# The gains of q and k as one column each, applied in the split of k behind its transpose

## The chip, the core and the metric

The kernel runs on one core of a Trainium2 chip, in one launch. The metric is the device time of one execution in microseconds (us). The engines are PE (TensorE, with a separate row for its weight loads, PEld), DVE (VectorE), ACT (ScalarE), POOL (GpSimd) and SP (SyncE, which here issues DMAs). PE's granted clock is full over the whole span.

## The reference, cut to what matters

One decoder layer: a modulated RMSNorm of x, a projection h @ w_in, two groups of attention heads, gates, an output projection and a residual. 512 tokens, model width 1024, head width 64, 8 query heads in each group A and B, 2 key heads in each branch.

```
def qk_norm(t, gain):
    tf = t.astype(jnp.float32)
    return tf * lax.rsqrt(jnp.mean(tf * tf, -1, keepdims=True) + EPS) * gain

qa = qk_norm(heads(q_a, A_HEADS), q_gain_a) * qscale       # qscale = 64 ** -0.5
ka = qk_norm(heads(k_a, A_KV), k_gain_a)
qb = qk_norm(heads(q_b, B_HEADS), q_gain_b) * qscale
k_cmp = qk_norm(compress_blocks(heads(kc, B_KV), ...), k_gain_cmp)
k_sel = qk_norm(heads(ks, B_KV), k_gain_sel)
k_win = qk_norm(heads(kw, B_KV), k_gain_win)
```

Only products of q and k are used afterwards (logits = q . k), so the gain of q, the gain of k and qscale can be put together as one vector of 64 numbers for each kind of key: four vectors, for window keys of group A, selected, window and compressed keys of group B. The kernel calls them kg and multiplies them into k alone.

## The kernel before, in words

All matrices are float32. For the large products the kernel splits each operand into a high part, rounded to the type float32r, and a low part (value minus high), and sums three products (high by high, high by low, low by high). ACT writes the high part, DVE subtracts to make the low part.

*Stage one, up to about 59 us.* x is loaded transposed, its norm and the modulation are made, and the projections of q, k, v of group A run on PE, k block by k block, while SP streams their weights through rings of four buffers (`ada_ring`, `wst_ring`). Between the loads of the first four blocks and those of the last four SP issues one load of small constants, the tile `rest` (L315). The instructions of this stage are held in the order in which they are written (`in_order`); at its end DVE makes `kg` from the gains (L429 to L434) and the negated sinks `nsink` (L435).

*Stage two.* The other projections (kv_cmp, kv_sel, kv_win_g, q_b, then the z gates) run on PE as a stream of small units, and between them stand slots of attention: scores (`slot_scores`, L882), a maximum and exponential (DVE L887, ACT L894), a scaling, a transpose (L930, L940), and the product with v (L957). The matrix instructions of the slots and of the compression MLP are chained in a fixed order. For the rest the compiler's planner decides at compile time, from estimated costs, in which order each engine issues what it has; the order in the trace is therefore not the written order everywhere.

*The keys.* `k_scale` is called three times: for group A (ty 0, tile kT), for selected keys (ty 1) and window keys (ty 2, both in tile kTb). Its input has tokens on partitions. DVE multiplies by the reciprocal norm of each token and head (L548), then by kg (L550), PE transposes four blocks of 128 tokens into one bank of PSUM, so that the 64 dimensions of head group 0 lie on partitions 0 to 63 and those of group 1 on 64 to 127 (L554). For each group ACT writes the high part twice (L558), once on its own half of the partitions and once on the other, and DVE writes the low part twice (L560). 64 partitions by 512 columns each. In the trace the second group's ACT copies begin when the first group's DVE subtractions are through. `q_scale` does the same for q without a gain (L531 to L542).

*The compressed keys.* In `cmp_mlp` one DVE instruction multiplies the output of the MLP in PSUM by its reciprocal norm and by kg (L650), PE transposes it (L654), and DVE copies it out of PSUM into kTc (L656).

Behind stage two come the remaining slots with the z gates and then the output projection (L1028 to L1039), which PE ends.

Of the kernel before, what the change touches and what calls it, by code (L numbers as in the profile page):

```python
# [9 lines left out]
F32 = mybir.dt.float32  # L10
# [3 lines left out]
AF = mybir.ActivationFunctionType  # L14
OP = mybir.AluOpType
# [4 lines left out]
S, D, HD, NB = 512, 1024, 64, 4  # L20
# [61 lines left out]
def hybrid_layer_kernel(ctx, tc, A, out):  # L82
    nc = tc.nc
    PE, DVE, ACT, POOL, SP = nc.tensor, nc.vector, nc.scalar, nc.gpsimd, nc.sync
# [3 lines left out]
    con = ctx.enter_context(tc.tile_pool(name="con", bufs=1))  # L88
# [22 lines left out]

    first = con.tile([128, 168], F32, name="first")
    cT, prm, ident = first[:, 0:8], first[:, 8:40], first[:, 40:168]
    rest = con.tile([128, 960], F32, name="rest")
    sml, anti = rest[:, 0:416], rest[:, 416:544]
    pos = rest[:, 544:576].rearrange("p (a b) -> p a b", a=2)
    w2 = rest[:, 576:832].rearrange("p (a b d) -> p a b d", a=2, b=2)
    cmask = rest[:, 832:960].rearrange("p (a b) -> p a b", a=NB)
    qga, kga, qgb, kgs, kgw, kgc = (sml[:, 64 * i:64 * i + 64] for i in range(6))
    bnsa, sinks = sml[:, 384:408], sml[:, 408:416]  # L120
    ones = con.tile([128, 1], F32, name="ones")
    DVE.memset(ones, 1.0)

# [1 line left out]
    hl = [T2(F32R, f"hl{k}") for k in range(8)]  # L125
    gacc = con.tile([128, D], F32, name="gacc")
    line_d = dram.tile([2, 8, LINE], F32, name="line_d")
    kg = con.tile([128, 4, HD], F32, name="kg")
    nsink = con.tile([128, 8], F32, name="nsink")
    sc_col = con.tile([128, 8], F32, name="sc_col")  # L130
    prm1 = con.tile([128, 8], F32, name="prm1")
# [43 lines left out]
    def split_to(g, p, ahead):  # L175

        while split_done[0] < min(len(split_list), split_pos[g, p] + ahead + 1):
            n, q = split_list[split_done[0]]
            if not all((n, h) in raws for h in ((0, 1) if n in COL else (q // 2,))):
                break  # L180
            split(n, q)
            split_done[0] += 1
# [115 lines left out]
    with in_order(tc) as begun:  # L298
# [113 lines left out]
        for k in range(8):  # L412
# [6 lines left out]
            for n in range(3):  # L419
# [6 lines left out]
                    new_tile(m)  # L426
                if k >= 6 and n == 1:
                    split_to("kv_cmp", 2 * (k - 6) + 1, 0)
        DVE.tensor_tensor(kg[:, 0], qga, kga, op=OP.mult)  # L429
        DVE.tensor_tensor(kg[:, 1], qgb, kgs, op=OP.mult)  # L430
        DVE.tensor_tensor(kg[:, 2], qgb, kgw, op=OP.mult)
        DVE.tensor_tensor(kg[:, 3], qgb, kgc, op=OP.mult)
        DVE.tensor_scalar(kg[:, 0:3], kg[:, 0:3], -(HD ** -0.5), None, op0=OP.mult)
        DVE.tensor_scalar(kg[:, 3], kg[:, 3], HD ** -0.5, None, op0=OP.mult)  # L434
        DVE.tensor_scalar(nsink, sinks, -1.0, None, op0=OP.mult)  # L435

    mp = ctx.enter_context(tc.tile_pool(name="mp", bufs=1))
# [1 line left out]
    def W2(name, shape=(128, 512)):  # L439
        return mp.tile(list(shape), F32, name=name, tag="w2", bufs=5)  # L440
# [22 lines left out]
    def PT():  # L463
        return ps_t.tile([128, 512], F32, name="pt")
# [31 lines left out]
    @contextmanager  # L496
    def block():

        with in_order(tc, chain, PE.engine) as last:
            yield  # L500
        chain.update(last)


    HALF = (slice(0, 64), slice(64, 128))
    qs = {}
    kT = {}
# [16 lines left out]
    def rnorm(ssq, n):  # L523
        DVE.tensor_scalar(ssq, ssq, 1.0 / HD, EPS, op0=OP.mult, op1=OP.add)
        return rsqrt(ssq, n)
# [19 lines left out]
    def k_scale(ty, src, rn):  # L545

        kn = W2("kn", (128, 8, HD))
        DVE.tensor_tensor(kn, src.rearrange("p t (g d) -> p (t g) d", d=HD), rn[:, :, None].to_broadcast([128, 8, HD]),  # L548
                          op=OP.mult)
        DVE.tensor_tensor(kn, kn, kg[:, ty:ty + 1, :].to_broadcast([128, 8, HD]), op=OP.mult)  # L550
        yield 0.0
        pt = PT()
        for t in range(NB):
            PE.transpose(pt[:, t * 128:(t + 1) * 128], kn[:, 2 * t:2 * t + 2].rearrange("p g d -> p (g d)"), ident)  # L554
        for g in range(2):
            part, k = pt[HALF[g], :], kT[ty, g]
            for e in (g, 1 - g):
                ACT.activation(k[HALF[e], 0, :], part, AF.Copy)  # L558
            for e in (g, 1 - g):
                DVE.tensor_tensor(k[HALF[e], 1, :], part, k[HALF[g], 0, :].bitcast(F32), op=OP.subtract)  # L560
        yield 0.44

    rn_a = {}
# [38 lines left out]
    def cmp_mlp():  # L602
        ph = ps_s.tile([128, 512], F32, name="s")
        for half in range(2):
            for _ in range(WAIT_M[half]):
                yield 0.0
            with block():
                for ii in range(8 * half, 8 * half + 8):
                    for kv in range(2):
                        PE.matmul(ph[64 * kv:64 * kv + 64, 0:256], X[kv][:, half, :, :, ii % 8].rearrange("p g n -> p (g n)"),  # L610
                                  raws[f"cmp{kv}", ii // 4][:, ii % 4, :], start=ii == 0, stop=ii == 15,
                                  skip_group_check=True)
                    if ii % 4 == 3:
                        load_next()
                        load_next()
            yield 3.6
        th_ = W2("cth", (128, 256))
        ACT.activation(th_, ph[:, 0:256], AF.Tanh, scale=0.5)
        sh = W2("csh", (128, 256))
        DVE.scalar_tensor_tensor(sh, th_, 1.0, ph[:, 0:256], op0=OP.add, op1=OP.mult)  # L620
        yield 0.0
        pt = PT()
        for hc in range(2):
            PE.transpose(pt[:, 128 * hc:128 * hc + 128], sh[:, 128 * hc:128 * hc + 128], ident)
        sT = W2("csT", (128, 2, 64))
        sTv = W2("csTv", (128, 2, 2, 4, 32))
        ptv = pt[:, 0:256].rearrange("p (c n) -> p c n", c=2)
        ACT.activation(sT, ptv[:, :, 0:64], AF.Copy, scale=0.5)
        for hc in range(2):
            DVE.tensor_scalar(sTv[:, hc], ptv[:, hc, 64:128].rearrange("p (g n) -> p g n", g=2)[:, :, None, :]  # L630
                              .to_broadcast([128, 2, 4, 32]), 0.5, None, op0=OP.mult)
        yield 0.25
        po = ps_s.tile([128, 512], F32, name="s")
        for hc in range(2):
            PE.matmul(po[0:64, 0:64], sT[:, hc, :], w2[:, 0, hc, :], start=hc == 0, stop=hc == 1)
        pv = ps_s.tile([128, 512], F32, name="s")
        for g in range(2):
            for hc in range(2):
                PE.matmul(pv[:, 64 * g:64 * g + 64], sTv[:, hc, g].rearrange("p r n -> p (r n)"), w2[:, 1, hc, :],
                          start=hc == 0, stop=hc == 1)  # L640
        for g in range(2):
            vc[g] = mp.tile([128, HD], F32, name=f"vc{g}")
            ACT.activation(vc[g], pv[:, 64 * g:64 * g + 64], AF.Copy)
        kcn = mp.tile([64, 2, HD], F32, name="kcn")
        sq = mp.tile([64, HD], F32, name="kcsq")
        ssk = sm.tile([128, 1], F32, name="ssk")
        DVE.memset(ssk, 1.0)
        ACT.activation(sq, po[0:64, 0:64], AF.Square, accum_out=ssk[0:64, :])
        rn = rnorm(ssk, 1)
        DVE.scalar_tensor_tensor(kcn, po[0:64, None, 0:64].to_broadcast([64, 2, HD]), rn[0:64, :],  # L650
                                 kg[0:64, 3:4, :].to_broadcast([64, 2, HD]), op0=OP.mult, op1=OP.mult)
        yield 1.3
        pt = PT()
        PE.transpose(pt[:, 0:64], kcn.rearrange("p a d -> p (a d)"), ident[0:64, 0:64])  # L654
        kTc = mp.tile([128, 2, 32], F32, name="kTc")
        DVE.tensor_copy(kTc.rearrange("p g n -> p (g n)"), pt[:, 0:64])  # L656
        yield 0.1
        X["kTc"] = kTc

# [283 lines left out]
    po = {}  # L943
# [84 lines left out]
    for n in range(8):  # L1028
        xr = mp.tile([128, S], F32, name="xr", tag="qc", bufs=2)
        ACT.dma_start(xr, A["xT"][n])  # L1030
        b = PJ()
# [10 lines left out]
def _layout(inp):  # L1042

    g = lambda n: np.asarray(inp[n])
    a = {}
    cc = np.ascontiguousarray
# [23 lines left out]
    for n, name in enumerate(("w_cmp_k1", "w_cmp_v1")):  # L1070
        a[f"w_cmp{n}"] = cc(g(name)[0].reshape(4, 4, 128, 256).transpose(0, 2, 1, 3))
    eye = np.eye(128, dtype=np.float32)
    a["first"] = cc(np.concatenate([g("c").reshape(8, 128).T, g("b_ada").reshape(24, 128).T,
                                    g("norm_gain").reshape(8, 128).T, eye], axis=1))
    smalls = np.concatenate([g(n)[0] for n in ("q_gain_a", "k_gain_a", "q_gain_b", "k_gain_sel", "k_gain_win",
                                               "k_gain_cmp", "b_nsa_gate", "sinks")])
    pos = np.stack([g("cmp_pos_k")[0].reshape(16, 128), g("cmp_pos_v")[0].reshape(16, 128)]).transpose(2, 0, 1)
    w2 = np.stack([g("w_cmp_k2")[0].reshape(2, 128, 64), g("w_cmp_v2")[0].reshape(2, 128, 64)]).transpose(2, 0, 1, 3)
    t = np.arange(S).reshape(NB, 128).T[:, :, None]
    cmask = np.where(16 * np.arange(32)[None, None, :] + 31 <= t, 0.0, -BIG).astype(np.float32)  # L1080
    a["rest"] = cc(np.concatenate([np.broadcast_to(smalls, (128, 416)), eye[::-1], pos.reshape(128, -1),
                                   w2.reshape(128, -1), cmask.reshape(128, -1)], axis=1))
    dist = 511 - np.arange(LINE)
    bucket = np.searchsorted(BUCKET_STARTS, np.maximum(dist, 0), side="right") - 1
# [25 lines left out]
```

## Time and profile before

| | us |
|---|---|
| median of 3 timed runs | 323.44 (322.80 to 324.18) |
| the profiled execution | 322.34 |
| its span, first to last instruction | 320.6 |
| PE busy in the span | 311.4 |
| PEld busy | 256.1 |
| DVE busy | 234.9 |
| ACT busy | 195.8 |

A row of the profile names a line of the kernel (L550), the engine, the operation, and output<-input by the program's names with partitions x elements. Weight loads (PEld) run beside the matrix instructions of PE. Matrix instructions are pipelined, so a busy PE is not PE at its peak. What stands in brackets in a timeline is the idle time of that engine just before the instruction and the instruction that ended the wait.

### The profile page before, as it was taken

Reading aid. Unit: us, or ns where it says so; the run is one execution under the profiler, and the core shown is the slowest. Engines: PE = TensorE matmul, PEld = TensorE weight load, DVE = VectorE, ACT = ScalarE, POOL = GpSimd, SP = SyncE. Lnnn points to the kernel's source line nnn. Section 1 sums busy time; section 2 is a strip of 40 time slices with the busy share of each in tenths; the row PEclk is TensorE's granted clock in tenths of the full one; section 3 lists DMA queues with packets and bytes.
Section 4 is the critical chain, followed back from the end, with each engine's and each line's share of the span. In section 5 each row is a group of like instructions: output and inputs, shape, how many; then the busy total and the mean of one; then the engine's idle time right before and its main releaser. Section 6 shows DMA issues by size and latency. Waiting matters only on the chain.

```text
span 320.6 us, 5999 instructions
## 1 busy us (share of the span) xinstructions
PE 311.4 (97%) x2187; PEld 256.1 (80%) x2188; DVE 234.9 (73%) x688; ACT 195.8 (61%) x473; POOL 4.5 (1%) x22
## 2 busy tenths in 40 slices
PE   6999999999999999999999999999999999999995
PEld 2477878888898899999975888788788878778884
DVE  2656797999995467797886999999599688454220
ACT  4566544957895667786956867877676866432100
POOL 1000000000000000000000000000000000000000
PEclk9999999999999999999999999999999999999999
DMA  7999998500085444130130223426224213243201
GB/s 264 385 408 410 378 325 265 171 0 3 0 252 176 130 167 131 35 113 20 39 127 4 97 65 102 133 66 196 68 67 132 66 67 131 67 140 114 108 33 65
DMA packets 31060, 44.26 MB, mean 138 GB/s; under 512 B 1766, under 2 KB 23398, under 8 KB 31032
## 3 DMA queue, kind: packets, MB, share of 16 engines
q1 hardware_dynamic: 29880, 41.79, 38.6%
q10 hardware_dynamic: 1152, 2.10, 2.1%
q8 instruction: 17, 0.28, 0.4%
q14 instruction: 11, 0.09, 0.1%
HBM read 41.74 MB, written 2.14 MB: 137 GB/s over the span
## 4 chain that ended last, share of the span: by engine, by line
PE 84%; DVE 6%; ACT 5%; DMA 2%; issue 1%; SPq 1%; POOL 0%; ACTq 0%; POOLq 0%
PE pj L491 30%; PE pj L481 9%; PE sq L294 8%; PE po L957 8%; PE s L882 7%; PE pt L940 4%; PE skv L295 4%; PE pt L930 3%; PE s L610 2%; DMA raw<-in_bias 2%; PE pj L227 2%; PE po L963 1%; DVE qs L542 1%; ACT pa L894 1%; PE pj L258 1%
## 5 line engine op out<-in xcount | busy, mean ns | idle before, releaser
L169 ACT ACTIVATE wh<-raw 128x512 fp32r<-128x512 f32 (+1 forms) x52 | 31.2, 635 | 16.4 <-PE pj L491 10.7
L170 DVE TENSOR_TENSOR wl<-raw,wh 128x512 fp32r<-128x512 f32 (+1 forms) x52 | 34.8, 690 | 8.2 <-ACT wh L169 4.7
L481 PE MATMUL pj<-wh,hh 128*128 128x256 f32 (+1 forms) x128 | 36.9, 288 | 0.0
L481 PE MATMUL pj<-wl,hh 128*128 128x256 f32 (+1 forms) x128 | 36.8, 287 | 0.0
L481 PE MATMUL pj<-wh,hl 128*128 128x256 f32 (+1 forms) x128 | 36.6, 286 | 0.0
L894 ACT ACTIVATE pp<-pp,nm 128x256 f32<-128x256 f32 (+2 forms) x48 | 29.4, 613 | 9.2 <-DVE nm L887 8.8
L491 PE MATMUL pj<-hh,wh 128*128 128x512 f32 x80 | 32.2, 403 | 0.0
L491 PE MATMUL pj<-hl,wh 128*128 128x512 f32 x80 | 31.9, 399 | 0.0
L491 PE MATMUL pj<-hh,wl 128*128 128x512 f32 x80 | 31.8, 397 | 0.0
L887 DVE CUSTOM_DVE_ANT_0 pp<-s,bias 128x256 f32<-128x256 f32 (+2 forms) x48 | 25.8, 547 | 2.4 <-PE s L882 2.4
L491 PE MATMUL pj<-yl,wh 128*128 128x512 f32 x64 | 25.4, 397 | 0.0
L491 PE MATMUL pj<-yh,wh 128*128 128x512 f32 x64 | 25.4, 401 | 0.0
L491 PE MATMUL pj<-yh,wl 128*128 128x512 f32 x64 | 25.3, 395 | 0.0
L481 PEld LDWEIGHTS pj<-wh,hh 128*128 128x128 f32 x128 | 24.2, 189 | 0.3 <-issue 0.2
L481 PEld LDWEIGHTS pj<-wl,hh 128*128 128x128 f32 x128 | 24.2, 189 | 0.2 <-issue 0.2
L481 PEld LDWEIGHTS pj<-wh,hl 128*128 128x128 f32 x128 | 24.2, 189 | 0.0
L882 PE MATMUL s<-kTb,qs 128*128 128x256 f32 (+2 forms) x96 | 23.7, 358 | 0.0
L1038 DVE SCALAR_TENSOR_TENSOR fin<-pj,gate,xr 128x512 f32<-128x512 f32 x8 | 6.0, 750 | 23.9 <-PE pj L491 23.9
L915 DVE TENSOR_SCALAR pp<-pp,rr,grev 128x256 f32<-128x256 f32 (+2 forms) x48 | 21.5, 475 | 0.3
L941 ACT COPY ptT<-pt 128x384 f32<-128x384 f32 (+1 forms) x32 | 15.7, 528 | 6.8 <-PE pt L940 6.6
L491 PEld LDWEIGHTS pj<-hh,wh 128*128 128x128 f32 x80 | 15.1, 188 | 4.7 <-issue 2.0
L931 ACT COPY ptT<-pt 128x512 f32<-128x512 f32 (+1 forms) x28 | 15.4, 551 | 4.7 <-PE pt L930 4.4
(235 smaller groups left out, 718.9 us busy)
## 6 DMA issues: line engine op xcount, KB each, us to landing
ada_ring<-in_w_ada_ss SPq DMA_DIRECT2D x16, 512.0 KB, 8.1
raw<-in_w_cmp SPq DMA_DIRECT2D x8, 512.0 KB, 6.3
raw<-in_w_gate SPq DMA_DIRECT2D x8, 512.0 KB, 4.8
raw<-in_w_o SPq DMA_DIRECT2D x8, 512.0 KB, 3.9
wst_ring<-in_w_qkv_a SPq DMA_DIRECT2D x8, 384.0 KB, 10.3
xTp<-in_xT SPq DMA_DIRECT2D x8, 256.0 KB, 4.6
xr<-in_xT ACTq DMA_DIRECT2D x8, 256.0 KB, 2.8
bias<-line_d SPq DMA_DIRECT2D x8, 256.0 KB, 4.3
```

The source lines that it names most:

```text
L169: ACT.activation(wh, src, AF.Copy)
L170: DVE.tensor_tensor(wl, src, wh.bitcast(F32), op=OP.subtract)
L294: PE.matmul(pj_q[tb], lt, w[:, 0:512], start=f, stop=l, skip_group_check=True)
L481: PE.matmul(bank[:, t * n:(t + 1) * n], h[:, tb * 128:(tb + 1) * 128], w[:, k % 2, :], start=k == 0 and m == 0, stop=k == 7 and m == 2)
L491: PE.matmul(bank, w, h, start=k == 0 and m == 0, stop=k == 7 and m == 2)
L882: PE.matmul(ps, qs[h][:, 128 * i:128 * i + 128], k[:, hl_, lo:lo + w], start=hl_ == 0, stop=hl_ == 1)
L887: DVE.tensor_tensor_reduce(out=P[:, g, 0:w], in0=ps, in1=bt, scale=1.0, scalar=init, op0=OP.add, op1=OP.min, accum_out=nm[:, g:g + 1])
L894: ACT.activation(P[:, g, 0:e], P[:, g, 0:e], AF.Exp, bias=nm[:, g:g + 1], scale=-1.0, accum_out=dn[:, g:g + 1])
L915: DVE.tensor_scalar(v, v, rr[:, g:g + 1], gates[:, g, br:br + 1], op0=OP.mult, op1=OP.mult)
L931: ACT.copy(T[:, :, 0:nb, :], rev(pt[:, 0:2 * nb * 128].rearrange("p (g b q) -> p g b q", g=2, b=nb)))
L941: ACT.copy(T[:, 0:nb, :], rev(pt[:, 0:nb * 128].rearrange("p (b q) -> p b q", b=nb)))
L957: PE.matmul(o[64 * g:64 * g + 64, 128 * i:128 * i + 128], vb[:, 64 * g:64 * g + 64], sl["T"][g][:, b, :], start=first_of and b == 0, stop= ...
```

## The change

The gains come as columns: the host lays `rest` out with 584 instead of 960 numbers for each partition, four columns of q gains and four of k gains, each the 64 gains twice, one copy for each half of the partitions. kg becomes four columns instead of four rows of 64 repeated on all partitions. Two small DVE instructions make it. In `k_scale` the multiplication L550 goes; the two ACT copies take the column as a scale for each partition, and the two DVE subtractions become (transposed value times column) minus high. In `cmp_mlp` the gain goes from the instruction ahead of the transpose into the copy behind it.

```diff
-    rest = con.tile([128, 960], F32, name="rest")
...
-    qga, kga, qgb, kgs, kgw, kgc = (sml[:, 64 * i:64 * i + 64] for i in range(6))
-    bnsa, sinks = sml[:, 384:408], sml[:, 408:416]
+    rest = con.tile([128, 584], F32, name="rest")
+    bnsa, sinks, qgain, kgain = rest[:, 0:24], rest[:, 24:32], rest[:, 32:36], rest[:, 36:40]
...
-    kg = con.tile([128, 4, HD], F32, name="kg")
+    kg = con.tile([128, 4], F32, name="kg")
...
-        DVE.tensor_tensor(kg[:, 0], qga, kga, op=OP.mult)
-        DVE.tensor_tensor(kg[:, 1], qgb, kgs, op=OP.mult)
-        DVE.tensor_tensor(kg[:, 2], qgb, kgw, op=OP.mult)
-        DVE.tensor_tensor(kg[:, 3], qgb, kgc, op=OP.mult)
-        DVE.tensor_scalar(kg[:, 0:3], kg[:, 0:3], -(HD ** -0.5), None, op0=OP.mult)
-        DVE.tensor_scalar(kg[:, 3], kg[:, 3], HD ** -0.5, None, op0=OP.mult)
+        for c, sign in ((slice(0, 3), -1), (slice(3, 4), 1)):
+            DVE.scalar_tensor_tensor(kg[:, c], qgain[:, c], sign * HD ** -0.5, kgain[:, c], op0=OP.mult, op1=OP.mult)
...
-        DVE.tensor_tensor(kn, kn, kg[:, ty:ty + 1, :].to_broadcast([128, 8, HD]), op=OP.mult)
...
-            part, k = pt[HALF[g], :], kT[ty, g]
+            part, by, k = pt[HALF[g], :], kg[HALF[g], ty:ty + 1], kT[ty, g]
             for e in (g, 1 - g):
-                ACT.activation(k[HALF[e], 0, :], part, AF.Copy)
+                ACT.activation(k[HALF[e], 0, :], part, AF.Copy, scale=by)
             for e in (g, 1 - g):
-                DVE.tensor_tensor(k[HALF[e], 1, :], part, k[HALF[g], 0, :].bitcast(F32), op=OP.subtract)
+                DVE.scalar_tensor_tensor(k[HALF[e], 1, :], part, by, k[HALF[g], 0, :].bitcast(F32),
+                                         op0=OP.mult, op1=OP.subtract)
...
-        DVE.scalar_tensor_tensor(kcn, po[0:64, None, 0:64].to_broadcast([64, 2, HD]), rn[0:64, :],
-                                 kg[0:64, 3:4, :].to_broadcast([64, 2, HD]), op0=OP.mult, op1=OP.mult)
+        DVE.tensor_scalar(kcn, po[0:64, None, 0:64].to_broadcast([64, 2, HD]), rn[0:64, :], None, op0=OP.mult)
...
-        DVE.tensor_copy(kTc.rearrange("p g n -> p (g n)"), pt[:, 0:64])
+        DVE.tensor_scalar(kTc.rearrange("p g n -> p (g n)"), pt[:, 0:64], kg[:, 3:4], None, op0=OP.mult)
...
+    gains = np.stack([g(n)[0] for n in ("q_gain_a", "q_gain_b", "q_gain_b", "q_gain_b",
+                                        "k_gain_a", "k_gain_sel", "k_gain_win", "k_gain_cmp")], axis=1)
```

## Rows read from the trace of the kernel before

**Rows 1.** Page, parts 1 and 4: busy us (share) x instructions; shares of the chain

```profile
PE 311.4 (97%) x2187; PEld 256.1 (80%) x2188; DVE 234.9 (73%) x688; ACT 195.8 (61%) x473; POOL 4.5 (1%) x22
...
PE 84%; DVE 6%; ACT 5%; DMA 2%; issue 1%; SPq 1%; POOL 0%; ACTq 0%; POOLq 0%
```

**Rows 2.** Stretch, length, busy us of PE, PEld, DVE, ACT, POOL; clock, DMA share, GB/s

```profile
0.00:58.00 58.00, 54.44 (x349) 39.30 (x351) 38.58 (x99) 31.77 (x54) 1.42 (x6) 1.00 0.96 345
58.00:160.00 102.00, 100.22 (x783) 91.16 (x782) 81.57 (x255) 76.43 (x201) 3.11 (x16) 1.00 0.30 92
58.00:76.00 18.00, 17.63 (x98) 14.80 (x97) 17.48 (x44) 12.49 (x27) 0.55 (x4) 1.00 0.16 50
76.00:94.00 18.00, 17.31 (x136) 16.11 (x135) 16.85 (x47) 16.10 (x45) 1.15 (x5) 1.00 0.27 70
130.00:138.00 8.00, 7.74 (x64) 7.29 (x63) 6.32 (x18) 7.41 (x19) 0.19 (x1) 1.00 0.00 0
```

**Rows 3.** What the weight load waited for, 58 to 160 us: us, times, longest

```profile
PEld s L882 <- DVE nm L887: 1.7, 6, 0.5
...
PEld pt L930 <- ACT kr L777: 0.8, 1, 0.8
PEld s L882 <- ACT qs L541: 0.6, 1, 0.6
PEld pt L554 <- DVE kn L550: 0.6, 2, 0.3
PEld pt L930 <- ACT wh L169: 0.4, 1, 0.4
...
PEld pt L536 <- DVE qn L531: 0.2, 1, 0.2
```

**Rows 4.** DVE groups by line and shape: count | busy us, mean ns | idle before

```profile
L1038 DVE SCALAR_TENSOR_TENSOR fin<-pj,gate,xr 128x512 f32<-128x512 f32 x8 | 6.0, 750 | 23.9 <-PE pj L491 23.9
...
L560 DVE TENSOR_TENSOR kTb<-pt,kTb 64x512 fp32r<-64x512 f32 x8 | 5.5, 688 | 1.0 <-ACT kTb L558 1.0
...
L550 DVE TENSOR_TENSOR kn<-kn,kg 128x512 f32<-128x512 f32 x3 | 2.1, 689 | 0.1
...
L816 DVE SCALAR_TENSOR_TENSOR yf<-po,szb 128x512 f32<-128x512 f32 x2 | 1.4, 691 | 5.0 <-PE po L963 5.0
...
L650 DVE SCALAR_TENSOR_TENSOR kcn<-s,n_y,kg 64x128 f32<-64x128 f32 x1 | 0.3, 342 | 0.0
...
L656 DVE COPY kTc<-pt 128x64 f32<-128x64 f32 x1 | 0.2, 224 | 0.8 <-PE pt L654 0.8
```

**Rows 5.** ACT groups by line and shape, the same columns

```profile
L917 ACT ACTIVATE pa<-pa,rr 128x256 f32<-128x256 f32 x12 | 6.1, 509 | 1.1 <-DVE rr L911 1.0
...
L558 ACT ACTIVATE kTb<-pt 64x512 fp32r<-64x512 f32 x8 | 4.7, 592 | 3.1 <-PE pt L554 2.2 <-DVE kTb L560 0.7
...
L337 ACT ACTIVATE sq<-xTp 128x256 f32<-128x256 f32 x2 | 0.7, 408 | 0.0
```

**Rows 6.** Timeline of DVE: start, us, instruction [idle before, releaser]

```profile
58.94 0.22 DVE L429 TENSOR_TENSOR kg<-rest 128x64 f32<-128x64 f32 x1
...
59.75 0.16 DVE L435 TENSOR_SCALAR nsink<-rest 128x8 f32<-128x8 f32 x1
...
103.56 1.40 DVE L560 TENSOR_TENSOR kTb<-pt,kTb 64x512 fp32r<-64x512 f32 x2 [0.80 <-ACT kTb L558]
```

**Rows 7.** Timeline of the weight load at the second and third split

```profile
98.40 0.42 PEld L554 LDWEIGHTS pt<-first,kn 128*128 128x128 f32 x4 [0.33 <-DVE kn L550]
...
105.73 0.30 PEld L882 LDWEIGHTS s<-kT,qs 128*128 128x128 f32 x2 [0.28 <-DVE nm L887]
...
131.07 0.42 PEld L554 LDWEIGHTS pt<-first,kn 128*128 128x128 f32 x4
```

**Rows 8.** DMA issues of rest: count, KB each, median us to landing

```profile
rest<-in_rest SPq DMA_DIRECT2D x1, 480.0 KB, 10.7
```

**Rows 9.** Timeline of ACT at the third split

```profile
130.37 0.60 ACT L794 ACTIVATE pp<-pj 128x512 f32<-128x512 f32 x1 [2.98 <-PE pj L481]
```

More of the change, by code (lines that the diff above doesn't have):

```diff
@@ L113, in hybrid_layer_kernel @@
     cT, prm, ident = first[:, 0:8], first[:, 8:40], first[:, 40:168]
-    rest = con.tile([128, 960], F32, name="rest")
[L115 to L118, printed above, removed]
-    qga, kga, qgb, kgs, kgw, kgc = (sml[:, 64 * i:64 * i + 64] for i in range(6))
-    bnsa, sinks = sml[:, 384:408], sml[:, 408:416]
+    rest = con.tile([128, 584], F32, name="rest")
+    bnsa, sinks, qgain, kgain = rest[:, 0:24], rest[:, 24:32], rest[:, 32:36], rest[:, 36:40]
+    anti = rest[:, 40:168]
+    pos = rest[:, 168:200].rearrange("p (a b) -> p a b", a=2)
+    w2 = rest[:, 200:456].rearrange("p (a b d) -> p a b d", a=2, b=2)
+    cmask = rest[:, 456:584].rearrange("p (a b) -> p a b", a=NB)
     ones = con.tile([128, 1], F32, name="ones")
@@ L1074, in _layout @@
                                     g("norm_gain").reshape(8, 128).T, eye], axis=1))
-    smalls = np.concatenate([g(n)[0] for n in ("q_gain_a", "k_gain_a", "q_gain_b", "k_gain_sel", "k_gain_win",
-                                               "k_gain_cmp", "b_nsa_gate", "sinks")])
+    smalls = np.concatenate([g("b_nsa_gate")[0], g("sinks")[0]])
+    gains = np.stack([g(n)[0] for n in ("q_gain_a", "q_gain_b", "q_gain_b", "q_gain_b",
+                                        "k_gain_a", "k_gain_sel", "k_gain_win", "k_gain_cmp")], axis=1)
     pos = np.stack([g("cmp_pos_k")[0].reshape(16, 128), g("cmp_pos_v")[0].reshape(16, 128)]).transpose(2, 0, 1)
@@ L1080, in _layout @@
     cmask = np.where(16 * np.arange(32)[None, None, :] + 31 <= t, 0.0, -BIG).astype(np.float32)
-    a["rest"] = cc(np.concatenate([np.broadcast_to(smalls, (128, 416)), eye[::-1], pos.reshape(128, -1),
+    a["rest"] = cc(np.concatenate([np.broadcast_to(smalls, (128, 32)), np.concatenate([gains, gains]), eye[::-1], pos.reshape(128, -1),
                                    w2.reshape(128, -1), cmask.reshape(128, -1)], axis=1))
```

## The prediction

> **What bounds the kernel now.** I read the page first, then the busy time by stretch, then what the weight load of PE waits for, then single instructions. On the page [rows 1] PE is busy for 97% of the span and carries 84% of the chain that ended last; DVE is at 73%, ACT at 61%. All that the change edits runs between 58 and 160 us, so that stretch counts. There [rows 2] PE is busy for 100.22 of 102 us, but within it two stretches are different: from 58 to 76 us DVE is busy for 17.48 of 18.00 us and from 76 to 94 for 16.85, so beside PE a second engine is full. After that DVE has room. The waits of the weight load in 58 to 160 us [rows 3] are short: 1.7 us on the minima of the scores (nm), 0.8 on an eviction (kr), 0.6 on qs, 0.6 on kn, 0.4 on a weight split (wh), 0.2 on qn, together 4.3 us. This is all that a faster k preparation can give back there, and a slower one adds to the same list. The reader is to see that a change worth a couple of microseconds on DVE is here worth at most what stands in that list.
>
> **The change, part by part.**
>
> *Gains (kg).* Six DVE instructions, from 58.94 to 59.75 us [rows 6], 0.81 us, become two on three columns and one column. A tiny instruction beside them (nsink, eight columns) takes 0.16 us [rows 6]; two make 0.32. DVE gives back 0.49 us, at a place where it is full.
>
> *Second multiplication of kn (L550).* Three instructions of 0.689 us each go [rows 4]: 2.07 us of DVE.
>
> *Low half of the split (L560).* Twelve subtractions of 0.688 us become a multiply and subtract with a scalar for each partition. No row has that form at 64 partitions. The nearest is fin: the same operation out of PSUM with such a scalar and a second tensor in SBUF, 512 columns, 0.750 us; without it, with a constant, yf out of PSUM takes 0.691 [rows 4]. So each costs between 0.00 and 0.06 us more. I take fin's form, 12 x 0.062 = 0.74 us.
>
> *High half (L558).* Twelve ACT copies of 0.592 us get a scale for each partition. The nearest pair, both 128x256 and out of SBUF: 0.509 us with such a scale (L917), 0.408 without (L337) [rows 5]. The difference, 0.101 us, is my value, none at all is the lower bound: 12 x 0.101 = 1.21 us of ACT. The copies read PSUM, which the pair does not; I see no row that says the scalar costs more there.
>
> *kcn and kTc.* One operand goes from the 0.342 us instruction, and the 0.224 us copy gets a scalar (0.06 by the above) [rows 4]: between -0.1 and +0.1 us, taken as nothing. It is one pair, and no row of it stands in the list of waits [rows 3].
>
> *The load of rest.* It shrinks from 480 KB [rows 8] to 584/960 of that, 292 KB. At the 345 GB/s of the first 58 us [rows 2] the 188 KB are 0.56 us of transfer. I cost it at nothing: PE is busy there for 54.44 of 58 us, and what it needs is loaded ahead into rings of four. If that cover is gone, it is a gain of up to 0.56 us. Nothing is moved past on the SP queue; the same number of DMAs is issued.
>
> Sum by engine: DVE -0.49 - 2.07 + 0.74 = -1.82 us, ACT +1.21 us.
>
> Now the path. The split of k is serial: two ACT copies, two DVE subtractions, for one head group, then the same for the other, since the second ACT pair starts behind the first DVE pair. The DVE row at 103.56 shows the hand-over from ACT, with 0.80 us of idle DVE [rows 6]. It grows by 4 x 0.101 + 4 x 0.062 = 0.65 us, and loses 0.69 us in front. So the last piece of k comes when it came before (-0.04), the first group's 0.69 - 0.20 - 0.12 = 0.37 us sooner. The three splits differ in what PE waits for.
>
> *First split (58 to 76 us).* DVE is full; it gives back 0.49 + 0.69 - 0.25 = 0.93 us. The waits that this can shorten are kn (0.2 of its 0.6), qn, qs and, through the DVE queue, kr [rows 3], 1.8 us. ACT is busy for only 12.49 of 18 us [rows 2], so its 0.4 us more are hidden there. I take -0.6, between 0 and -0.93; behind it the next late things are the qs splits, on DVE and ACT in turn.
>
> *Second split (94 to 106 us).* PE's wait of 0.33 us for kn at 98.40 goes [rows 7]. But at 105.73 PE waits 0.28 us for the minimum of the scores [rows 7], which stands in the DVE queue behind the last pair of the split, and that pair waits for ACT [rows 6]. From the first pair to the last that queue grows by 0.20 + 0.12 + 0.12 = 0.44 us. Net +0.1, between -0.33 and +0.44. This is where a gain is given back.
>
> *Third split (130 to 138 us).* Here the transpose at 131.07 waits for nothing [rows 7], so the removed 0.69 us is hidden already. ACT is busy for 7.41 of 8.00 us [rows 2], in a run that begins at 130.37 after 2.98 us of idle [rows 9], and at its end PE waits 0.4 us for wh [rows 3]. The split puts 4 x 0.101 = 0.40 us into that run. An earlier kn lets ACT start it sooner, so I take half: +0.2, between -0.2 and +0.5.
>
> Sum: -0.6 + 0.1 + 0.2 = -0.3 us. With the ends: 0 + 0.44 + 0.5 = +0.9 above, -0.93 - 0.33 - 0.2 - 0.56 = -2.0 below. The profiled execution took 322.34 us (span 320.6 and 1.74 around it); it would be 322.0. It lies below all three timed runs (322.80 to 324.18), so I set the difference against their median: 323.44 - 0.3 = 323.1 us.
>
> A rule that bears on which engine is the bound: the Trainium skill, Perfetto Trace Analysis, Identifying the Most-Contended Engine, says that the busy share of matmuls is a poor measure of PE, that the share of weight loads is the one to take, and that the engine with the highest share is to be optimised first. By it DVE leads in both stretches from 58 to 94 us, and its saving would count in full there. The traces so far bear this out in part: weight loads are busy for 14.80 and 16.11 of 18 us, less than DVE [rows 2].
>
> **The rivals.**
>
> *DVE paces the stage (faster).* Every DVE microsecond saved shortens the end: 323.44 - 1.82 = 321.6. For it: the DVE shares of 97 and 94% [rows 2]. Against: over 58 to 160 us DVE is busy for 81.57 of 102 us, and PE's waits on kn and qn are 0.8 us in all [rows 2, 3].
>
> *The split is the path (slower).* PE waits at the end of each split and what L550 gives back is lost before it (as in the third split, where PE comes later than kn). Then each split costs its 0.65 us: 3 x 0.65 = +1.95, 325.4 us. It decides where the nm wait behind each split grows by the whole 0.65; two splits of three give only +1.3. For it: the waits of 0.28 us at 105.73 and on wh [rows 3, 7]. Against: 0.69 us go from the same chain.
>
> *Another order.* The order of DVE and ACT behind 58 us is made at compile time from estimated costs; six groups of instructions change theirs, so it can come out differently, with other waits. Price: half of the 4.3 us [rows 3] gone or half again as much, 2.1 us: 321.3 or 325.5. The profile of before tells nothing of which.
>
> **How the numbers follow.** About 0.5%, 1.6 us, is what a measurement of this kernel can tell from no change. My forecast has 0.47 and a range of its own of 321.9 to 324.4. DVE as the pace has 0.20; at -1.82 it lies just past the limit, so 0.13 faster, 0.07 same. The split as the path has 0.08: 0.05 slower, 0.03 same. Another order has 0.25: 0.14 faster, 0.10 slower, 0.01 same. Together faster 0.27, same 0.47 + 0.07 + 0.03 + 0.01 = 0.58, slower 0.15. The range goes from 321.0 to 325.1, which takes in the rivals' near ends.
>
> **What would show it.** Right: L550 is gone; L558 stands near 0.69 us and L560 near 0.75; PE's waits on kn vanish at the first two splits; the nm wait behind the second split grows; DVE's busy time falls by about 1.8 us, ACT's rises by 1.2, PE's stays within a few tenths. Wrong: L558 or L560 unchanged in length, or the weight-load waits of 58 to 160 us changing by over 1.5 us in sum, which would be another order or DVE as the pace.

## The result, and the profile after

The changed kernel took 325.65 us (median of six runs, 324.64 to 327.00), the kernel before, run beside it, 323.79 us (322.80 to 325.87). The ratio is 1.0059, 95% interval 1.0030 to 1.0087: slower by 1.9 us, and above the predicted range. The profiled execution of the changed kernel took 326.35 us, its span is 324.3 us.

The prices of the single instructions came as worked out, and the time did not. First the pages and groups that answer to those of before. In the changed file most lines stand 1 to 6 lower: L560 is L554, L558 is L552, L169 is L168, L887 is L881, L930 is L924, L491 is L486.

The page of the changed kernel, parts 1 and 4 [rows 1]:

```profile
PE 315.5 (97%) x2187; PEld 257.6 (79%) x2188; DVE 233.9 (72%) x681; ACT 198.2 (61%) x473; POOL 4.5 (1%) x22
...
PE 73%; DVE 9%; ACT 7%; DMA 7%; issue 2%; SPq 1%; ACTq 0%
```

Its busy time by stretch, the columns of [rows 2], with one stretch more (10 to 20 us):

```profile
0.00:58.00 58.00, 54.73 (x337) 38.88 (x339) 36.56 (x95) 29.60 (x51) 1.42 (x6) 0.97 0.92 333
58.00:160.00 102.00, 100.33 (x780) 90.42 (x779) 78.96 (x243) 77.45 (x200) 3.10 (x16) 1.00 0.31 97
10.00:20.00 10.00, 8.21 (x49) 4.66 (x50) 5.71 (x21) 4.54 (x11) 0.00 (x0) 0.84 0.98 381
58.00:76.00 18.00, 17.68 (x93) 14.40 (x92) 17.30 (x40) 14.79 (x31) 0.43 (x3) 1.00 0.24 78
```

What its weight load waited for from 58 to 160 us [rows 3]:

```profile
PEld s L876 <- DVE nm L881: 2.3, 9, 0.3
...
PEld s L876 <- ACT qs L536: 0.5, 1, 0.5
PEld pt L924 <- ACT pa L911: 0.4, 1, 0.4
...
PEld pt L548 <- DVE kn L543: 0.2, 1, 0.2
PEld pt L744 <- DVE gsig L742: 0.2, 1, 0.2
```

DVE and ACT groups [rows 4, 5], and the DMA of rest [rows 8]:

```profile
L1032 DVE SCALAR_TENSOR_TENSOR fin<-pj,gate,xr 128x512 f32<-128x512 f32 x8 | 6.0, 751 | 18.3 <-PE pj L486 18.3
L554 DVE SCALAR_TENSOR_TENSOR kTb<-pt,kg,kTb 64x512 fp32r<-64x512 f32 x8 | 6.0, 750 | 2.6 <-ACT kTb L552 2.4
...
L645 DVE TENSOR_SCALAR kcn<-s,n_y 64x128 f32<-64x128 f32 x1 | 0.3, 344 | 0.0
L650 DVE TENSOR_SCALAR kTc<-pt,kg 128x64 f32<-128x64 f32 x1 | 0.3, 284 | 0.9 <-PE pt L648 0.9
...
L552 ACT ACTIVATE kTb<-pt,kg 64x512 fp32r<-64x512 f32 x8 | 5.5, 683 | 1.0 <-PE pt L548 0.6 <-DVE kTb L554 0.3
...
rest<-in_rest SPq DMA_DIRECT2D x1, 292.0 KB, 9.4
```

The subtraction costs 750 ns instead of 688 (+62, as priced), the copy 683 instead of 592 (+91, priced at 101). L550 is gone, and no wait of the weight load is put down to kn at the first two splits any more. The weight load is idle there all the same, ahead of the same transposes (before: 0.24 and 0.33 us, put down to kn):

```profile
67.46 0.42 PEld L548 LDWEIGHTS pt<-first,kn 128*128 128x128 f32 x4 [0.39 <-issue]
...
99.60 0.42 PEld L548 LDWEIGHTS pt<-first,kn 128*128 128x128 f32 x4 [0.33 <-DVE pa L913]
```

The waits on nm rose from 1.7 us in 6 waits to 2.3 in 9, and two places wait that did not before: the transpose of gsig (L744), and kn at the third split.

The next view is the weight split, which the change does not edit: a copy on ACT that makes the high part of a weight tile for each large product. All its 52 instructions, before and after, with the idle time of ACT ahead of them:

```profile
L169 ACT ACTIVATE wh<-raw 128x512 fp32r<-128x512 f32 (+1 forms) x52 | 31.2, 635 | 16.4 <-PE pj L491 10.7 <-DMA xr<-in_xT 2.2 <-DMA raw<-in_w_z_a 2.0
```

```profile
L168 ACT ACTIVATE wh<-raw 128x512 fp32r<-128x512 f32 (+1 forms) x52 | 31.5, 634 | 24.2 <-PE pj L486 14.9 <-DVE fin L1032 6.9 <-DMA raw<-in_w_z_b 1.5
```

The same copies now find ACT waiting 24.2 us instead of 16.4: 14.9 for products on PE, and 6.9 for the final DVE instruction (fin), which has nothing to do with a weight. Waits of these two kinds are waits for places. The compiler gives tiles that don't live at the same time the same bytes of SBUF, and the later writer waits until the earlier tile is read. How many places a name has can be counted in the compiled programs (the experiments are told below):

| | before, e10 | changed | e7 | e4, e8 | e9 |
|---|---|---|---|---|---|
| places of the 52 wh tiles | 15 | 12 | 11 | 15 | 12 |
| of them back in the place of the wh four tiles earlier | 17 | 25 | 27 | 17 | 16 |
| places of the 18 pa tiles (attention scores) | 5 | 3 | 3 | 5 | 5 |
| places of the 8 xr tiles | 6 | 2 | 2 | 6 | 6 |
| waits on semaphores in the program | 1561, 1563 | 1602 | 1630 | 1545, 1539 | 1537 |

A copy that makes wh waits for the product that reads the wh whose place it takes. And xr, an operand of fin, is loaded by DMAs that ACT issues: with two places the third load stands in ACT's queue until fin has read the first xr, and the weight split stands behind it.

The sum of 24.2 us must not be taken for the loss. 18.3 us of it, the waits for fin among them, stand behind 250 us (before: 12.8 of the 16.4), and there PE falls only 0.25 us further behind, by the weight loads matched as below. Most of the loss arises between 58 and 145 us. In that stretch three copies wait, 0.99, 0.33 and 0.41 us, all for products on PE; in the kernel before none does.

How far PE falls behind can be read by matching each weight load of a kernel with the same one of before. The table gives, for all kernels run, the median difference of their starts in us within four stretches of before, less the difference at 54 to 60 us (the column "start", which the change does not touch). Where PE has another order (changed, e1, e3, e4, e8, e9, e12), a load can come earlier or later for that alone; so 86 to 90 us counts only loads ahead of which both kernels have issued the same loads. The last columns are the timed ratio and its interval.

| kernel | start | 86-90 | 120-126 | 138-144 | 210-216 | ratio | 95% |
|---|---|---|---|---|---|---|---|
| changed (above) | 2.17 | -0.05 | 0.31 | 1.06 | 1.05 | 1.0059 | 1.0030-1.0087 |
| e1 changed again | 0.57 | -0.02 | 0.32 | 1.04 | 1.05 | 1.0050 | 1.0024-1.0076 |
| e2 changed, order and sizes of before | 0.17 | 0.17 | 0.58 | 0.99 | 1.00 | 1.0038 | 1.0013-1.0063 |
| e3 before, order of changed | 0.46 | 0.94 | 1.19 | 1.37 | 1.43 | 1.0034 | 1.0014-1.0053 |
| e4 changed, sizes of before | 0.74 | -0.19 | -0.19 | 0.13 | 0.15 | 1.0013 | 0.9982-1.0045 |
| e5 L550 removed alone | 2.01 | -0.38 | -0.36 | -0.37 | -0.34 | 0.9977 | 0.9952-1.0003 |
| e6 scalar operands alone | 1.97 | 0.36 | 0.86 | 1.39 | 1.54 | 1.0052 | 1.0027-1.0078 |
| e7 before, rest 1024 wide | 1.11 | -0.01 | 0.18 | 0.91 | 0.99 | 1.0051 | 1.0025-1.0077 |
| e8 changed, rest 776 wide | -0.11 | -0.16 | -0.19 | 0.16 | 0.15 | 1.0009 | 0.9988-1.0031 |
| e9 changed, rest 1024 wide | 3.06 | -0.13 | -0.14 | 0.20 | 0.35 | 1.0021 | 0.9996-1.0047 |
| e10 before, rest 992 wide | -0.17 | 0.00 | 0.00 | 0.02 | 0.05 | 0.9993 | 0.9972-1.0015 |
| e11 ACT scalar alone | 0.75 | 0.11 | 0.27 | 0.46 | 0.47 | 1.0004 | 0.9979-1.0029 |
| e12 first split alone | 2.59 | 0.03 | 0.01 | 0.02 | 0.09 | 0.9995 | 0.9970-1.0021 |

The start differs by -0.2 to +3.1 us from execution to execution, whatever the kernel. A single time is therefore a poor witness here; the columns behind it agree between two executions of the changed kernel to 0.03 us. (Near 222 us these two differ by 0.4 us, so the table ends ahead of it.)

### The profile page after: what moved, and what is told of

It reads as the page before. It is cut to its first block, busy times and chain, and to the rows that moved or that the text cites. A ratio compares the mean times of both kernels' runs of the same rounds, so it can differ in the third digit from the quotient of the medians.

```text
span 324.3 us, 6016 instructions
## 1 busy us (share of the span) xinstructions
PE 315.5 (97%) x2187; PEld 257.6 (79%) x2188; DVE 233.9 (72%) x681; ACT 198.2 (61%) x473; POOL 4.5 (1%) x22
## 4 chain that ended last, share of the span: by engine, by line
PE 73%; DVE 9%; ACT 7%; DMA 7%; issue 2%; SPq 1%; ACTq 0%
PE pj L486 26%; PE sq L293 7%; PE pj L476 7%; PE po L951 6%; PE s L876 6%; PE skv L294 3%; PE pt L934 3%; DMA raw<-in_w_z_b 3%; PE pt L924 3%; PE s L605 2%; DMA ada_ring<-in_w_ada_ss 2%; DVE qs L537 2%; DMA xTp<-in_xT 2%; ACT wh L168 1%; PE pj L226 1%
## 5 line engine op out<-in xcount | busy, mean ns | idle before, releaser
L168 ACT ACTIVATE wh<-raw 128x512 fp32r<-128x512 f32 (+1 forms) x52 | 31.5, 634 | 24.2 <-PE pj L486 14.9
L169 DVE TENSOR_TENSOR wl<-raw,wh 128x512 fp32r<-128x512 f32 (+1 forms) x52 | 35.2, 691 | 14.9 <-ACT wh L168 9.6
L888 ACT ACTIVATE pp<-pp,nm 128x256 f32<-128x256 f32 (+2 forms) x48 | 29.4, 614 | 8.4 <-DVE nm L881 8.0
L486 PE MATMUL pj<-hh,wh 128*128 128x512 f32 x80 | 32.5, 407 | 0.0
L486 PE MATMUL pj<-hl,wh 128*128 128x512 f32 x80 | 32.0, 400 | 0.0
L486 PE MATMUL pj<-hh,wl 128*128 128x512 f32 x80 | 31.7, 396 | 0.0
L881 DVE CUSTOM_DVE_ANT_0 pp<-s,bias 128x256 f32<-128x256 f32 (+2 forms) x48 | 25.8, 548 | 2.0 <-PE s L876 1.9
L486 PE MATMUL pj<-yh,wh 128*128 128x512 f32 x64 | 25.5, 404 | 0.0
L486 PE MATMUL pj<-yl,wh 128*128 128x512 f32 x64 | 25.4, 398 | 0.0
L486 PE MATMUL pj<-yh,wl 128*128 128x512 f32 x64 | 25.3, 395 | 0.0
L476 PEld LDWEIGHTS pj<-wh,hh 128*128 128x128 f32 x128 | 24.2, 189 | 0.5 <-issue 0.3
L1032 DVE SCALAR_TENSOR_TENSOR fin<-pj,gate,xr 128x512 f32<-128x512 f32 x8 | 6.0, 751 | 18.3 <-PE pj L486 18.3
L486 PEld LDWEIGHTS pj<-hh,wh 128*128 128x128 f32 x80 | 15.0, 188 | 4.7 <-issue 2.0
```

Of the source, the lines that this page charges most:

```text
L168: ACT.activation(wh, src, AF.Copy)
L169: DVE.tensor_tensor(wl, src, wh.bitcast(F32), op=OP.subtract)
L476: PE.matmul(bank[:, t * n:(t + 1) * n], h[:, tb * 128:(tb + 1) * 128], w[:, k % 2, :], start=k == 0 and m == 0, stop=k == 7 and m == 2)
L486: PE.matmul(bank, w, h, start=k == 0 and m == 0, stop=k == 7 and m == 2)
L881: DVE.tensor_tensor_reduce(out=P[:, g, 0:w], in0=ps, in1=bt, scale=1.0, scalar=init, op0=OP.add, op1=OP.min, accum_out=nm[:, g:g + 1])
L888: ACT.activation(P[:, g, 0:e], P[:, g, 0:e], AF.Exp, bias=nm[:, g:g + 1], scale=-1.0, accum_out=dn[:, g:g + 1])
```

## The experiments

e1 to e4 were put to four theories. START: the loss is in the first 20 us. ORDER: the planner issues the instructions of DVE, ACT and PE in another order. PRICE: the scalar operands cost on the path what the removal does not return. PLACE: rest and kg are smaller, so other tiles lie at other addresses and wait for one another.

**e1.** The changed kernel again, unaltered.

> The changed kernel once more, beside the others of this call, with the span and clock of each execution. Every theory expects a ratio to the kernel before of 1.004 to 1.008 (measured: 1.0059). Theory START (the difference is made in the first 20 us by loads that land late, not by the change): it is within 1.003, and executions with a full clock are as fast as before.

324.19 us against 322.78, ratio 1.0050. Its start is 0.57 us late instead of 2.17, and the loss behind 58 us is the same. START expected a ratio within 1.003. It explains a part of the 326.35 us of the execution profiled first, and nothing of the loss behind 58 us.

**e2.** The change, with the order of every engine held to that of before, and rest and kg as large as before.

```diff
-    rest = con.tile([128, 584], F32, name="rest")
+    rest = con.tile([128, 960], F32, name="rest")[:, 0:584]
-    kg = con.tile([128, 4], F32, name="kg")
+    kg = con.tile([128, 4, HD], F32, name="kg")[:, :, 0]
...
+    pinned(tc, ORDER)   # each engine issues in the order of before
```

> The change, but every engine's instructions held in the order of the kernel before, and the tiles rest and kg held at their old sizes in SBUF (their new contents fill a part of them), so that the other tiles lie where they lay. Theory ORDER (the new order costs it): ratio 0.997 to 1.001. Theory PRICE (a scalar for each partition makes the split of k later): ratio 1.004 to 1.007. Theory PLACE (the smaller tiles put other tiles elsewhere, and they then wait for one another): 0.997 to 1.001. START: 1.000.

1.0038, just under what PRICE expected: in the old order the edit alone costs 1.00 us: 0.17 at the first split, 0.41 at the second, 0.41 at the third.

**e3.** The kernel before, held to the order of the changed one.

> The kernel before, with its own instructions and sizes, held in the order of the changed kernel (the second multiplication of kn right behind the first). Theory ORDER: ratio 1.004 to 1.008, as the changed kernel. PRICE, PLACE and START: 0.999 to 1.001.

1.0034, 1.43 us, of which 0.94 stand by the first split. The new order is worse for the old instructions. It is not worse for the new ones, as the next run shows: the planner's order fits what it orders.

**e4.** The change in its own order, with the two size lines of e2 alone.

> The change with the tiles rest and kg at their old sizes in SBUF; the order is the changed kernel's own. ORDER and PRICE: ratio 1.004 to 1.007. PLACE: 0.997 to 1.001. START: 1.000.

1.0013, and 0.15 us behind 58 us: with the old sizes 0.90 of e1's 1.05 us are gone. The interval overlaps that of e1; the matched loads tell them apart. That leaves PLACE as the main cause, and asks for PLACE without the change (e7).

**e5 and e6** split the edit of e2. e5 leaves L550 out and puts nothing in its place; e6 keeps L550 and gives the copies and subtractions a column of ones.

```diff
-        DVE.tensor_tensor(kn, kn, kg[:, ty:ty + 1, :].to_broadcast([128, 8, HD]), op=OP.mult)
```

```diff
-                ACT.activation(k[HALF[e], 0, :], part, AF.Copy)
+                ACT.activation(k[HALF[e], 0, :], part, AF.Copy, scale=ones[HALF[g]])
-                DVE.tensor_tensor(k[HALF[e], 1, :], part, k[HALF[g], 0, :].bitcast(F32), op=OP.subtract)
+                DVE.scalar_tensor_tensor(k[HALF[e], 1, :], part, ones[HALF[g]], k[HALF[g], 0, :].bitcast(F32),
+                                         op0=OP.mult, op1=OP.subtract)
```

> The kernel before, in its own order of instructions and with its own tile sizes, without the second multiplication of kn (L550) and nothing put in its place: k of all three kinds lacks the gain. It splits what the whole edit cost in that order (e2, ratio 1.0038, +0.84 us behind 58 us). RETURNED (the removal gives back what the prediction said, -0.4 at the first split, -0.33 at the second, 0 at the third, and the scalar operands then cost +1.6): -0.7 us, ratio 0.998. HIDDEN (nothing waits for kn that doesn't next wait for something else): 0 to -0.2 us, ratio 0.9995 to 1.000; PE's waits on kn are gone from the trace all the same.

> The kernel before, in its own order of instructions, with L550 kept, and with a scalar for each partition (a column of ones) in the twelve ACT copies and the twelve DVE subtractions; rest takes 1036 instead of 960 columns of SBUF so that the program has about as many waits as before (1567 against 1561). RETURNED: +1.5 us, ratio 1.0047 (the rival 'The split is the path' priced it at 3 x 0.65 = 1.95, ratio 1.006). HIDDEN: the same as the whole edit in that order, +0.8 us, ratio 1.0025.

e5 0.9977, e6 1.0052. The removal returns 0.38 us at the first split and nothing at the other two; the operands cost 0.36, 0.50 and 0.53 us. Both together are 1.20 us, 0.20 above e2: e6 has the numbers of places of e9 (12, 5, 6), which costs e9 the same 0.20 over e8, so its cost is to be read as 1.3 to 1.5 us. RETURNED stands for the operands, and half of it for the removal: the second split gave nothing. Its row shows why. e5's weight load there, and DVE's multiplication (L611 is L548) that makes kn:

```profile
100.03 0.42 PEld L616 LDWEIGHTS pt<-first,kn 128*128 128x128 f32 x4 [0.33 <-issue]
```

```profile
98.31 0.69 DVE L611 TENSOR_TENSOR kn<-kr,n_y 128x512 f32<-128x512 f32 x1
```

kn is now complete at 99.00, 1.03 us ahead of the transpose, and the 0.33 us of idle time stands there as before. In [rows 7] it was put down to kn, which ended last there; it is a gap that the weight load leaves at this place in any case, in the changed kernel too (0.33 us at 99.60, above).

**e7 and e8** are PLACE by itself: one number in the kernel before, and one in the changed kernel.

```diff
-    rest = con.tile([128, 960], F32, name="rest")
+    rest = con.tile([128, 1024], F32, name="rest")[:, 0:960]
```

```diff
-    rest = con.tile([128, 584], F32, name="rest")
+    rest = con.tile([128, 776], F32, name="rest")[:, 0:584]
```

> The kernel before with one number changed: rest takes 1024 columns of SBUF, of which 960 are used. The load, every instruction and their order on each engine are the same; the tiles of the later stages come to lie at other addresses, and the program has 1630 waits on semaphores instead of 1561 (among them 13 more of ACT's and 18 more of DVE's weight splits on PE). PLACE: the loss that the change showed beyond e4, +0.8 to +1.3 us, shows here without the change: ratio 1.0025 to 1.004. Rival, that places cost nothing: 1.000, within 0.001.

> The change word for word, but rest takes 776 instead of 584 columns of SBUF, of which 584 are used: the same load, instructions and order as the changed kernel, and 1539 waits instead of 1602. PLACE: as e4, ratio 1.0013 (+0.4 us). Rival, that the smaller load or kg's size made the rest of the loss: as e1, ratio 1.005.

e7 1.0051, e8 1.0009: PLACE at both ends. kg keeps its four columns in e8, so its size had no part. The wait is seen on one weight split near 124 us. ACT in the kernel before, then in e7, which issues the same instructions in the same order:

```profile
123.24 0.59 ACT L931 COPY ptT<-pt 128x512 f32<-128x512 f32 x1 [0.40 <-PE pt L930]
123.72 0.63 ACT L169 ACTIVATE wh<-raw 128x512 fp32r<-128x512 f32 x1
```

```profile
124.53 0.59 ACT L931 COPY ptT<-pt 128x512 f32<-128x512 f32 x1 [0.41 <-PE pt L930]
125.53 0.63 ACT L169 ACTIVATE wh<-raw 128x512 fp32r<-128x512 f32 x1 [0.41 <-PE pj L481]
```

And the same pair, with DVE's half of the split behind it, in e8 and in the changed kernel:

```profile
123.42 0.63 ACT L168 ACTIVATE wh<-raw 128x512 fp32r<-128x512 f32 x1
...
124.08 0.69 DVE L169 TENSOR_TENSOR wl<-raw,wh 128x512 fp32r<-128x512 f32 x1 [0.26 <-ACT wh L168]
```

```profile
126.72 0.63 ACT L168 ACTIVATE wh<-raw 128x512 fp32r<-128x512 f32 x1 [0.41 <-PE pj L476]
...
127.39 0.69 DVE L169 TENSOR_TENSOR wl<-raw,wh 128x512 fp32r<-128x512 f32 x1 [0.79 <-ACT wh L168]
128.00 0.48 DVE L881 CUSTOM_DVE_ANT_0 pa<-s,bias,nsink 128x256 f32<-128x256 f32 x1
...
129.88 0.30 PEld L744 LDWEIGHTS pt<-gsig,rest 128*128 128x128 f32 x2 [0.18 <-DVE gsig L742]
```

In the two kernels that lose, the copy waits 0.41 us for a product on PE; in the other two it follows at once. DVE, which issues in order, waits 0.53 us longer for wh (0.79 less 0.26), the minimum of the scores and gsig come later behind it, and there PE waits. Matched load by load, the changed kernel loses to e8 0.13 us up to 108 us, 0.36 at 108 to 118, 0.30 at 126 to 131, and 0.11 more by 140. From 60 to 160 us copies of wh wait in the changed kernel, e1 and e7, and in none of the others.

The largest of these steps, at 108 to 118 us, has no weight split in it. There an exponential of attention scores (L888) starts late behind the minimum that it takes (L881). In e8, then in the changed kernel:

```profile
110.40 0.35 DVE L881 CUSTOM_DVE_ANT_0 pa<-s,bias,nsink 128x128 f32<-128x128 f32 x1
110.85 0.41 ACT L888 ACTIVATE pa<-pa,nm 128x129 f32<-128x129 f32 x1
```

```profile
112.91 0.35 DVE L881 CUSTOM_DVE_ANT_0 pa<-s,bias,nsink 128x128 f32<-128x128 f32 x1
113.64 0.40 ACT L888 ACTIVATE pa<-pa,nm 128x129 f32<-128x129 f32 x1 [0.42 <-DVE nm L881]
```

From the end of the minimum to the exponential it is 0.10 us in e8 and 0.38 in the changed kernel. e1 and e7 have 0.38 and 0.39, all other kernels 0.10 or 0.11. The three that are late are the three in which pa has three places instead of five; what holds the exponential there is not shown.

**e9 and e10** ask whether it is the place or the width. The changed kernel gets 1024 columns, which cost the kernel before 1.6 us; the kernel before gets 992.

```diff
-    rest = con.tile([128, 584], F32, name="rest")
+    rest = con.tile([128, 1024], F32, name="rest")[:, 0:584]
```

```diff
-    rest = con.tile([128, 960], F32, name="rest")
+    rest = con.tile([128, 992], F32, name="rest")[:, 0:960]
```

> The change word for word, but rest takes 1024 instead of 584 columns of SBUF, of which 584 are used; same load, instructions and order; 1537 waits instead of 1602. 1024 columns cost the kernel before +1.6 us (e7). PLACE (what counts is where the other tiles come to lie and so the waits, not the size itself): as e8, ratio 1.000 to 1.002, and no weight split waits for the output tile fin. Rival, that a tile of 1024 columns is itself the cost: ratio 1.005.

> The kernel before with rest taking 992 instead of 960 columns of SBUF: 1563 waits instead of 1561 (e7, 32 columns more, has 1630). PLACE: no change, ratio 1.000 within 0.002. Rival, that any wider tile costs: ratio 1.002 to 1.005.

e10 is the kernel before in every column. e9's interval reaches 1.0047 and alone would not decide; its trace does: 0.35 us behind 58 us, no weight split waits for fin, and none waits at all from 60 to 160 us. What the copies waited for from 58 to 325 us, in e9 and then in e7:

```profile
ACT wh L168 <- PE pj L486: 15.5, 7, 5.9
ACT wh L168 <- DMA raw<-in_w_z_a: 1.9, 1, 1.9
ACT wh L168 <- DMA raw<-in_w_z_b: 0.7, 1, 0.7
```

```profile
ACT wh L169 <- PE pj L491: 16.6, 9, 3.5
ACT wh L169 <- DVE fin L1038: 6.8, 2, 3.8
```

So 1024 columns are bad in one kernel and good in the other, and 32 columns decide in the kernel before (e10, e7). What counts is the packing that comes out.

**e11 and e12.** e11 is e6 without the DVE part. e12 makes the change at the first split alone (ty 0), with L550 kept for ty 1 and 2; it is the version that the runs so far pointed to.

```diff
-        DVE.tensor_tensor(kn, kn, kg[:, ty:ty + 1, :].to_broadcast([128, 8, HD]), op=OP.mult)
+        if ty:
+            DVE.tensor_tensor(kn, kn, kg[:, ty:ty + 1, :].to_broadcast([128, 8, HD]), op=OP.mult)
...
-                ACT.activation(k[HALF[e], 0, :], part, AF.Copy)
+                ACT.activation(k[HALF[e], 0, :], part, AF.Copy, scale=1.0 if ty else kga0[HALF[g]])
```

> The kernel before in its own order and sizes, with L550 kept, and the scalar for each partition in the twelve ACT copies alone; the DVE subtractions stay plain (1566 waits). Of the cost of both (e6, +1.53 us behind 58 us, three steps of 0.35, 0.49 and 0.45) the twelve ACT copies have 12 x 0.092 = 1.10 of 1.84 us. SERIAL (both kinds count by their length, since the split is a chain of both): +0.9 us, ratio 1.003. Rival, that only what lies in DVE's queue counts, since PE waits for the minimum of the scores behind the split: +0.2 us, ratio 1.0005.

> The change at the first split alone, the place where DVE is full and removal gave something back (e5, -0.36): kn of group A without L550, the scalar in its four ACT copies and four DVE subtractions; selected, window and compressed keys as before. The planner's own order, 1568 waits. By the steps of e5 and e6 at that split (-0.36 and +0.35) nothing is left: ratio 1.000. If the planner's new order keeps the -0.5 that e4 had by 80 to 95 us and loses nothing later: 0.998. If the order costs what the new order did with the old instructions (e3): 1.003.

e11: 0.47 us of e6's 1.3 to 1.5, less than SERIAL and more than its rival. The ACT copies are 60% of the added length (1.10 of 1.84 us) and about a third of the cost; by difference, since the DVE part was not run alone, an added DVE microsecond cost more than an ACT one. e12: 0.9995, nothing left, as the steps of e5 and e6 say. (The -0.5 that its expectation takes from e4 comes from loads in another order; counted as in the table it is -0.19.) No version run beats the kernel before by more than can be measured.

## Why the prediction was wrong

**The step that failed: the load of rest.** The prediction costed the smaller tile as 188 KB less to transfer, "at nothing", and so it was (e8, which loads the 292 KB, is 0.11 us ahead of the kernel before at 58 us, less than two executions differ). That the tile is also smaller in SBUF, and that every later tile is packed around it, stood in no step and no rival. It is the larger part of the loss: e1 against e4 on the same chip is 1.0050 against 1.0013, with medians of 324.19 and 323.38 us, 0.8 us apart; in the traces it is 0.90 of 1.05 us. e7 shows the same 0.99 us without the change. That the loss goes by way of the weight split is shown for one split and for PE's waits behind it; the largest step, 0.36 us, has no split in it. How the 0.9 us divide between wh and pa was not tried; e9, with 12 places for wh and the old number for the others, has little of it. xr has no part in it: the waits for fin come at 286 to 300 us.

**Another order** came nearest, priced at +2.1 us. The order did change, but it was no loss: old instructions lose 1.43 us in it, new ones 0.85 less than in the old order (0.15 against 1.00). The sign set for it, waits in the weight load's list changing by over 1.5 us, did not show either: the named waits of 58 to 160 us sum to 4.5 us before and 4.3 after, those without a releaser ("issue") to 1.9 and 2.7.

**The edit itself** (e8, own order, good places) was forecast at -0.3 and measured +0.15 behind 58 us, 1.0009 in time, inside what was called no change:

- First split, -0.6: -0.16 in e8, -0.05 in the changed kernel. This is the second step that failed, a term sized too large. The waits on kn, qn, qs and kr that a relieved DVE was to shorten were 0.24, 0.18, 0.58 and 0.78 us; in e8 the weight load is idle for 0.48, 0.22, 0.41 and 0.74 us at the four places that answer to them. In the old order the removal returned 0.38 us (e5), and the operands took 0.36 of it (e6).
- Second split, +0.1: -0.03. In the old order the price behind the split is there, 0.50 in e6 with 0.44 predicted, and the -0.33 against it did not exist, since the gap at 98.40 was no wait on kn. In e8's own order the price does not show; that the sum came near is luck.
- Third split, +0.2: +0.34. "Hidden already" holds for L550 (e5: 0.00); the split cost 0.53 alone (e6) where half of 0.40 was taken.
- Instruction prices: +62 ns was exact, +101 was +91. A rule agrees here: the Trainium skill, ScalarE: Activation LUTs, What ACT_TABLE_LOAD costs, gives about 93 ns for each operand that is one value per partition; 592 to 683 ns is 91, out of PSUM. DVE's busy time fell by 1.0 us (234.9 to 233.9), 1.5 in e8 (233.4), with 1.8 predicted; ACT's rose by 2.4 (1.4 in e8) with 1.2 predicted, and PE's by 4.1 (0.3 in e8) where a few tenths were said.

**DVE paces the stage** fell in e5, which takes 2.07 us from DVE and returns 0.34. The Trainium skill's rule is that the engine with the highest occupancy is to be optimised first (Perfetto Trace Analysis, Identifying the Most-Contended Engine). How much of a saving returns it does not say: at the first split, where DVE was full, e5 returned 0.38 of 0.69 us. Another sentence of the Trainium skill (Perfetto Trace Analysis, Optimization Strategy) is nearer to the cause: the same gap, repeated on the engine that should be saturated, can mean that there isn't enough SBUF for the next tile. Here such gaps stood on ACT, ahead of the weight splits (0.99, 0.33 and 0.41 us), and not on the engine that was full.

**The split is the path** had each split at 0.65 us. e6 has 0.36, 0.50 and 0.53, 1.39 in sum with 1.95 said; with the removal beside them it is e2's 1.00.

## What to carry to other kernels

Where the compiler packs SBUF, a tile's size is an input to the schedule: when a change alters one, build the change once with the tile padded to its old size, and compare the places and waits of the two programs, before the instructions are blamed. In a list of waits, a wait put down to the instruction that ended last may be a gap that stays when that instruction is early; check how long before the gap's end it was done. When two kernels are compared load by load and their orders differ, compare only where both have done the same work. A price on two engines in a chain is not cancelled by an equal saving ahead of the chain when the saving was already hidden.

## What the runs showed that was not expected

The first 20 us of PE vary by themselves. In the profiled execution of the changed kernel the granted clock was 0.84 from 10 to 20 us, in e9 0.80, in e8 1.00, and the first two start late, as e5 does, which loads rest as before:

```profile
10.00:20.00 10.00, 8.94 (x49) 4.78 (x49) 5.71 (x20) 5.19 (x11) 0.00 (x0) 0.80 1.00 386
```

```profile
10.00:20.00 10.00, 9.07 (x68) 4.93 (x71) 7.08 (x22) 6.55 (x13) 0.00 (x0) 1.00 1.02 394
```

The first is e9, the second e8. The 0.80 and 0.84 are means over a stretch in which the clock stood at its full level, 2.4 GHz, for a part and at 1.2 GHz for the rest; the changed kernel's PE had been busy for 8.57 of the 10 us ahead of it. In the first 58 us its weight load waited 1.6 us for the first weights (ada_ring), in e9 0.9, in e8 0.6. By 58 us e9 is 3.06 us behind the kernel before, the changed kernel 2.17, and e8 0.11 ahead. The five executions that start 2 us late or more (changed, e5, e6, e9, e12) have such a stretch at 1.2 GHz (0.80 to 0.89 from 10 to 20 us), the others are at 1.00. The timed medians of e8 and e9 (323.52 and 323.54 us) show nothing of it, so it belongs to the execution and not to the kernel.
